# Input projection of a decoder trunk: both activation parts in one matmul stream, token scale folded into the operands, x and z in turn

## The chip, the cores and the metric

One core of one Trainium2 chip runs the whole program. The metric is device time in microseconds for one execution; three executions of the kernel before gave a median of 2697.6 us (2697.39 to 2698.57).

## What is computed

The reference is a two-layer decoder trunk over 256 tokens of width 2048: a Mamba-2 (SSD) mixer, a SwiGLU FFN, a dilated-window attention mixer and a second FFN, each behind an RMS norm and with a residual add. The change touches the first matrix product alone:

```python
h = rms_norm(x, mix_norm[0])          # x * gain * rstd(token)
proj = h @ w_in                       # 2048 -> 4096 (z) + 6144 (x, B, C) + 64 (dt)
xbc = silu(causal_depthwise_conv(proj_xbc, conv_w, conv_b))   # width 4
dt = softplus(dt_raw + dt_bias)
y = ssd_chunked(xs * dt, dt * a, b, c) + xs * d
y = group_rms_norm(y * silu(z), norm_w) @ w_out
```

## The kernel before, in words

**Number format.** Every fp32 operand is held as two fp32r parts, high and low. A product is weight-high times activation-high, weight-high times activation-low and weight-low times activation-high. Activations stand transposed, 128 channels by 256 tokens; `XT` holds the 16 blocks of 128 channels in 8 operand tiles, each block as `[high, low]` side by side, 512 columns in all.

**Weights.** They come from memory in tiles of 128x2048, each used as two *halves* of 1024 columns. `split` (line 145) makes a half's high part with a cast on ScalarE (ACT) and its low part with a subtraction on VectorE (DVE). There are four buffers for high and four for low parts, and `next_half` (line 160) splits three halves ahead. So while TensorE (PE) begins half n, the split of half n+3 is queued; its low part needs the buffer that half n-1 has just left. There are 914 halves, of which the input projection uses 162: 20 for each of the 8 head groups and 2 for `dt`.

**Products.** `t_unit`/`t_units` (lines 222 to 248) run 24 matmuls of 256 columns for a half (16 with the high weights, once for each activation part, and 8 with the low ones). `p_unit` (line 250) runs 8 matmuls of 512 columns, both activation parts in one stream, and 8 of 256; its two sums stand apart in PSUM, and `joined` (line 270) copies one on ACT and adds the other on DVE. Before the change p_units are used in both FFNs and in part of the output projections. Each unit has one of two PSUM accumulators: `begin_unit` (line 199) forces the evacuation of the unit two back.

**Order of the projection** (lines 633 to 643). Group g runs `bc` (B and C, 4 halves), in group 0 also `dt` (2 halves), then x (8 halves) and z (8 halves). The operands are x times gain, without the token scale `rb`, which is known only after the sum of squares; so every evacuation multiplies by `rb` on DVE (`scaled`, line 392).

**The rest is background work.** Evacuations, convolution (`first_tap` on ACT, `taps` on DVE, `half_tanh` on ACT, `gate` on DVE), the scan (`ssd`, line 532) and the group norm are Python generators in three queues: 0 for the evacuations and convolutions, 1 for norms, 2 for `dt` and `ssd`. After each half, `Background.step` (line 68) goes through the queues in that order and advances each by one `yield`, but only while its debt is low. The debt is counted in planner units, 0.1 plus elements/960 for a DVE instruction and 0.1 plus elements/1200 for an ACT one: 0.37 and 0.31 at 256 elements, 0.63 and 0.53 at 512. A step pays off 1.3 for DVE and 1.4 for ACT; a queue is passed over while the debt is above three quarters of these (0.975 for DVE). `Background.need` (line 74) advances all queues whatever the debt, until a wanted key is done. Splits are not counted in the debt. All engines take their instructions in the order in which the program wrote them.

```python
def step(self, free=False):
    self.debt = [max(d - s, -1.4) for d, s in zip(self.debt, self.SHARE)]
    for q in self.queues:
        if free or all(d < 0.75 * s for d, s in zip(self.debt, self.SHARE)):
            self.advance(q)
```

In the output projection the last group's operands are due 28 halves after the end of the input projection (`OUT0`, line 895).

Of the kernel before, what the change touches and what calls it, by code (L numbers as in the profile page):

```python
# [10 lines left out]
F32 = mybir.dt.float32  # L11
F32R = mybir.dt.float32r
AF = mybir.ActivationFunctionType
OP = mybir.AluOpType
AX = mybir.AxisListType

P = 128
S = 256
# [67 lines left out]
def trunk_kernel(  # L86
# [21 lines left out]
    def slot(shape, dt=F32):  # L108
        return slots.tile(shape, dt, tag="slot", bufs=28, name=name("slot"))
# [8 lines left out]
    def tmp(shape, dt=F32):  # L118
        return small.tile(shape, dt, tag="tmp", bufs=6, name=name("tmp"))
# [11 lines left out]
    bg = Background(3, (V, A))  # L131
# [115 lines left out]
    def t_unit(ncols, X, xkey, evac, q=0):  # L247
        t_units([(0, range(16))], ncols, 16, X, xkey, [evac], q)

    def p_unit(nk, X, xkey, evac):  # L250


        u, ps = begin_unit()
        for k0 in range(0, nk, 4):
            h, l = next_half(256)
            ks = range(k0, k0 + 4)
            for k in ks:
                bg.need((xkey, k // 2))
            for k in ks:
                for m in range(2):  # L260
                    T.matmul(ps[:, m], h[:, k % 4, m * P:(m + 1) * P], X[k], start=(k == 0), stop=False,  # L261
                             skip_group_check=True)
            for k in ks:
                for m in range(2):
                    T.matmul(ps[:, m, 0], l[:, k % 4, m * P:(m + 1) * P], X[k][:, 0, :], start=False,  # L265
                             stop=(k == nk - 1), skip_group_check=True)
            bg.step()
        bg.add(0, evac(ps, u))

    def joined(ps):  # L270
# [7 lines left out]
    XT = {}  # L278
# [60 lines left out]
    def clear_norm():  # L339
        bg.done -= {("XT", j) for j in range(8)} | {"rstd"}  # L340
        XT.clear()
# [10 lines left out]
    def t_residual(nb, gcol):  # L352
        def gen(ps, u):
            for b in range(2):
                k = 4 * nb + 2 * b
                V.tensor_tensor(xt[:, k:k + 2, :], ps[:, b], xt[:, k:k + 2, :], OP.add)
            bg.done.add(("evac", u))
            yield
            yield from after_residual((2 * nb, 2 * nb + 1), gcol)
        return gen  # L360
# [16 lines left out]
    def prep():  # L377
        for nb in range(4):
            for pair in (2 * nb, 2 * nb + 1):
                gained(pair, 0)  # L380
            add_squares()
            for pair in (2 * nb, 2 * nb + 1):
                squares(pair)
            yield
        yield from finish_norm()
        V.tensor_scalar(cwb, cwb, 0.5, None, OP.mult)
        A.activation(hpar[64:128, 1:2], hpar[64:128, 1:2], AF.Exp)
        V.tensor_scalar(hpar[64:128, 1:2], hpar[64:128, 1:2], -1.0, None, OP.mult)
        V.memset(hpar[0:64, 1:2], 1.0)
        bg.done.add("prep")  # L390

    def scaled(sums):
        u = tmp([P, 2, S])
        V.tensor_tensor(u, sums, rb[:, None, :].to_broadcast([P, 2, S]), OP.mult)
        return u

    def dt_evac(ps, u):
# [47 lines left out]
    def first_tap(u, dst, cts):  # L445

        for m, ct in enumerate(cts):
            A.activation(dst[:, m, :], u[:, m, :], AF.Identity, scale=cwb[:, 144 + ct:145 + ct],
                         bias=cwb[:, 192 + ct:193 + ct])

    def taps(u, dst, cts, js):
        for j in js:
            d = 3 - j
            for m, ct in enumerate(cts):
                V.scalar_tensor_tensor(dst[:, m, d:], u[:, m, :S - d], cwb[:, j * 48 + ct:j * 48 + ct + 1],
                                       dst[:, m, d:], OP.mult, OP.add)

    def half_tanh(v, scale):
        th = tmp([P, 2, S])
        A.activation(th, v, AF.Tanh, scale=scale)  # L460
        return th

    def gate(out_, th, v):
        V.scalar_tensor_tensor(out_, th, 1.0, v, OP.add, OP.mult)

    def bc_evac(g):
        def gen(ps, u):
            v = scaled(ps[:, :, 0])
            bg.done.add(("evac", u))
            yield  # L470
            both, cts = slot([P, 1024]), (32 + g, 40 + g)
            bc = both[:, 0:512].rearrange("p (a t) -> p a t", t=S)
            first_tap(v, bc, cts)
            yield
            taps(v, bc, cts, (2, 1))
            yield
            taps(v, bc, cts, (0,))
            yield
            th = half_tanh(bc, 1.0)
            yield  # L480
            gate(bc, th, bc)
            BC[g] = bc, both[:, 512:896]
            yield
        return gen

    def x_evac(g):
        def gen(ps, u):
            xs = slot([P, 4, S])
            d0, d1 = xs[:, 0:2, :], xs[:, 2:4, :]
            c0, c1 = (4 * g, 4 * g + 1), (4 * g + 2, 4 * g + 3)  # L490
            v0 = scaled(ps[:, 0])
            yield
            first_tap(v0, d0, c0)
            v1 = scaled(ps[:, 1])
            bg.done.add(("evac", u))
            yield
            taps(v0, d0, c0, (2, 1))
            first_tap(v1, d1, c1)
            yield
            taps(v0, d0, c0, (0,))  # L500
            taps(v1, d1, c1, (2,))
            yield
            th = half_tanh(d0, 1.0)
            taps(v1, d1, c1, (1, 0))
            yield
            gate(d0, th, d0)
            th = half_tanh(d1, 1.0)
            yield
            gate(d1, th, d1)
            XS[g] = xs  # L510
            bg.add(2, ssd(g))
        return gen

    def z_evac(g):
        def gen(ps, u):
            sz = slot([P, 4, S])
            v0 = scaled(ps[:, 0])
            yield
            t0 = half_tanh(v0, 0.5)
            v1 = scaled(ps[:, 1])  # L520
            bg.done.add(("evac", u))
            yield
            gate(sz[:, 0:2, :], t0, v0)
            t1 = half_tanh(v1, 0.5)
            yield
            gate(sz[:, 2:4, :], t1, v1)
            SZ[g] = sz
        return gen

    BC, XS, SZ, Y = {}, {}, {}, {}  # L530

    def ssd(g):
# [100 lines left out]
    bg.add(0, prep())  # L633
    bg.need(("XT", 1))
    for g in range(NG):
        t_unit(256, XT, "XT", bc_evac(g))
        if g == 0:
            t_unit(128, XT, "XT", dt_evac, 2)
        t_unit(512, XT, "XT", x_evac(g))
        t_unit(512, XT, "XT", z_evac(g))  # L640
    bg.need("rstd")
    bg.need(("evac", units[0] - 1))
    clear_norm()
    t_units(OUT0, 512, 32, Y, "Y", [t_residual(nb, 32) for nb in (0, 1)])
    for pair in range(4, 8):
        p_unit(32, Y, "Y", p_residual(pair, 32))
# [255 lines left out]
def _weights(i):  # L902


    w_in, w_out = np.asarray(i["ssm_w_in"])[0], np.asarray(i["ssm_w_out"])[0]
    w_qkv, a_out = np.asarray(i["attn_w_qkv"])[0], np.asarray(i["attn_w_out"])[0]
    gate, up, down = (np.asarray(i[n]) for n in ("ffn_w_gate", "ffn_w_up", "ffn_w_down"))
    halves = []

    def put(ks, *blocks):  # L910

        n = sum(b[2] for b in blocks)
        kk = 1024 // n
        for k0 in ks[::kk]:
            halves.append((k0, kk, blocks))

    r16 = range(16)
    for g in range(NG):
        put(r16, (w_in, 8192 + g * P, P), (w_in, 9216 + g * P, P))
        if g == 0:  # L920
            put(r16, (w_in, 10240, 64), (w_in, 10240, 64))
        put(r16, (w_in, 4096 + g * 512, 512))
        put(r16, (w_in, g * 512, 512))

    def put_out(w, order, nk):
        for j, ks in order:
            put(ks, (w, j * 512, 512))
        for pair in range(4, 8):
            put(range(nk), (w, pair * 256, 256))

    def put_ffn(l):
        for j in range(44):
            put(r16, (gate[l], j * P, P), (up[l], j * P, P))
        for pair in range(8):
            put(range(44), (down[l], pair * 256, 256))

    put_out(w_out, OUT0, 32)
    put_ffn(0)
    for hf, g, kind in QKV:
        put(r16, (w_qkv, ((g * 3 + kind) * 8 + hf * 4) * P, 512))  # L940
    put_out(a_out, OUT1, 8)
    put_ffn(1)
    packed = np.empty((len(halves) // 2, P, 2048), np.float32)
    for j, (k0, kk, blocks) in enumerate(halves):
        dst = packed[j // 2, :, (j % 2) * 1024:(j % 2 + 1) * 1024].reshape(P, kk, 1024 // kk)
        c = 0
        for w, c0, n in blocks:
            dst[:, :, c:c + n] = w[k0 * P:(k0 + kk) * P, c0:c0 + n].reshape(kk, P, n).transpose(1, 0, 2)
            c += n
    assert len(halves) % 2 == 0  # L950
    return packed
# [60 lines left out]
```

## Time and profile before

| what | value |
|---|---|
| median of three runs | 2697.6 us |
| profiled execution, its own time | 2698.51 us |
| its span, first to last instruction | 2696.4 us |
| TensorE busy | 2673.5 us (99%) |
| VectorE busy | 1700.7 us (63%) |
| ScalarE busy | 1326.3 us (49%) |
| mean granted TensorE clock | 0.999 |

2.1 us of the profiled execution lie outside its span. A busy PE says only that matmuls were in flight; how many were started in a stretch says more. In a timeline, the first column is the start in us, the second the length, and what stands in brackets is how long the engine was idle before and what ended that.

### The profile page before, as it was taken

To read this page: it belongs to the slowest core of one execution; us is meant where nothing else is said; L and a number is where in the kernel's file an instruction comes from. 1 tells how busy PE (TensorE), PEld (TensorE's weight loads), DVE (VectorE), ACT (ScalarE), POOL (GpSimd) and SP (SyncE) were. 2 spreads that over 40 slices of the span, in tenths; PEclk is the share of its full clock that TensorE was granted. 3 is DMA by queue.
4 is the path that set the end of the run, shared out by engine and by line. 5 is a ranking of instruction groups with operands and counts; after the bars stand their busy time and mean duration, and the time that the engine had idled before them with its cause. 6 is when DMAs were issued, how large, how long until landed. Compare 5 with 4: busy or idle time off the path is not lost.

```text
span 2696.4 us, 40315 instructions
## 1 busy us (share of the span) xinstructions
PE 2673.5 (99%) x16460; PEld 2391.9 (89%) x16460; DVE 1700.7 (63%) x2104; ACT 1326.3 (49%) x1947; POOL 199.8 (7%) x215
## 2 busy tenths in 40 slices
PE   7999999999999999999999999999999999999999
PEld 7999999999888888888888888888888888888888
DVE  6777777756566666665555777766666666665444
ACT  5666666654454444444444555544454444444332
POOL 1011111110000000000001330220000000000000
PEclk9999999999999999999999999999999999999999
DMA  5454555545555555555555554553455555555553
GB/s 222 178 184 175 187 179 189 177 177 187 188 188 188 188 188 187 189 189 193 190 189 203 183 186 152 185 185 141 156 188 188 188 188 188 188 188 194 197 198 128
DMA packets 71432, 495.75 MB, mean 184 GB/s; under 512 B 8320, under 2 KB 8704, under 8 KB 13008
## 3 DMA queue, kind: packets, MB, share of 16 engines
q1 hardware_dynamic: 68400, 483.81, 49.5%
q0 software_dynamic: 2848, 9.37, 1.1%
q8 instruction: 129, 2.11, 0.3%
q14 instruction: 55, 0.45, 0.1%
HBM read 490.99 MB, written 2.16 MB: 183 GB/s over the span
## 4 chain that ended last, share of the span: by engine, by line
PE 98%; ACT 1%; issue 0%; DVE 0%; POOL 0%; DMA 0%; SPq 0%; ACTq 0%; POOLq 0%
PE acc L261 39%; PE acc L240 21%; PE acc L265 20%; PE acc L217 15%; PE bg L588 1%; PE bg L754 0%; PE bg L787 0%; PE bg L860 0%; PE bg L549 0%; ACT wh L38 0%; ACT slot L38 0%; PE bg L324 0%; PE bg L784 0%; PE bg L862 0%; DMA xres<-in_x_dram 0%
## 5 line engine op out<-in xcount | busy, mean ns | idle before, releaser
L38 DVE TENSOR_TENSOR wl<-w,wh 128x1024 fp32r<-128x1024 f32 x914 | 1128.3, 1236 | 904.7 <-ACT wh L38 903.7
L38 ACT CAST wh<-w 128x1024 fp32r<-128x1024 f32 x914 | 955.5, 1047 | 1089.8 <-PE acc L261 507.2
L261 PE MATMUL acc<-slot,wh 128*128 128x512 f32 x4416 | 1106.7, 392 | 2.1 <-DVE xres L38 1.7
L261 PEld LDWEIGHTS acc<-slot,wh 128*128 128x128 f32 x4416 | 794.2, 189 | 145.1 <-issue 2.7
L265 PEld LDWEIGHTS acc<-slot,wl 128*128 128x128 f32 x4416 | 602.4, 190 | 43.0
L265 PE MATMUL acc<-slot,wl 128*128 128x256 f32 x4416 | 615.7, 282 | 0.0
L240 PE MATMUL acc<-slot,wh 128*128 128x256 f32 x3232 | 430.1, 286 | 12.8 <-ACT wh L38 10.7
L240 PEld LDWEIGHTS acc<-slot,wh 128*128 128x128 f32 x3232 | 404.8, 193 | 19.9 <-ACT wh L38 10.8
L217 PE MATMUL acc<-wh,slot 128*128 128x512 f32 x1152 | 290.5, 394 | 0.0
L217 PEld LDWEIGHTS acc<-wh,slot 128*128 128x128 f32 x1152 | 213.7, 188 | 43.2
L240 PE MATMUL acc<-slot,wl 128*128 128x256 f32 x1616 | 226.8, 283 | 0.9 <-DVE wl L38 0.9
L240 PEld LDWEIGHTS acc<-slot,wl 128*128 128x128 f32 x1616 | 208.6, 192 | 1.1 <-DVE wl L38 1.1
L217 PE MATMUL acc<-wl,slot 128*128 128x512 f32 x576 | 154.2, 389 | 0.0
L217 PEld LDWEIGHTS acc<-wl,slot 128*128 128x128 f32 x576 | 108.1, 188 | 22.7
L38 ACT ACTIVATE tmp<-tmp 128x256 f32<-128x256 f32 (+1 forms) x104 | 46.8, 450 | 163.9 <-DVE tmp L38 163.6
L284 POOL TENSOR_TENSOR tmp<-tmp 128x256 f32<-128x256 f32 x32 | 27.6, 868 | 1022.1 <-ACT tmp L38 1017.0
L38 ACT ACTIVATE wide<-tmp,bias 128x128 f32<-128x128 f32 x192 | 62.9, 391 | 13.9 <-PE bg L588 9.4
L38 DVE SCALAR_TENSOR_TENSOR slot<-tmp,vec,slot 128x255 f32<-128x255 f32 (+1 forms) x144 | 67.6, 528 | 0.0
L38 DVE TENSOR_TENSOR tmp<-tmp 128x256 f32<-128x256 f32 x88 | 37.4, 425 | 42.6 <-ACT tmp L38 42.6
L38 DVE TENSOR_TENSOR tmp<-acc,tmp 128x512 f32<-128x512 f32 x88 | 60.1, 683 | 4.0 <-ACT tmp L38 4.0
L38 DVE TENSOR_TENSOR tmp<-tmp,rb 128x512 f32<-128x512 f32 x88 | 60.3, 686 | 0.1
L38 ACT ACTIVATE tmp<-slot 128x128 f32<-128x128 f32 (+1 forms) x136 | 52.7, 394 | 14.9 <-DVE slot L38 13.8
(131 smaller groups left out, 1191.3 us busy)
## 6 DMA issues: line engine op xcount, KB each, us to landing
w<-in_weights_dram SPq DMA_DIRECT2D x455, 1024.0 KB, 4.8
tmp<-acum POOLq DMA_DIRECT2D x32, 256.0 KB, 4.6
xres<-in_x_dram SPq DMA_DIRECT2D x4, 512.0 KB, 7.8
w<-in_weights_dram SPq DMA_DIRECT2D x4, 512.0 KB, 8.4
out_dram<-xres SPq DMA_DIRECT2D x8, 256.0 KB, 2.2
slot<-in_mask_dram POOLq DMA_DIRECT2D x1, 384.0 KB, 5.6
slot<-in_q_norm_dram POOLq DMA_DIRECT2D x1, 192.0 KB, 5.6
slot<-in_k_norm_dram POOLq DMA_DIRECT2D x1, 192.0 KB, 7.5
```

The costliest lines, as they stand in the source:

```text
L38: return call(out, *args, **kw)
L217: T.matmul(ps[tb], X[k][:, part, tb * P:(tb + 1) * P], w[:, k % 2, :], start=(k == 0 and i == 0), stop=(k == 15 and i == 2))
L240: T.matmul(pss[j][:, b, c, :], w[:, k % kk, m * P:(m + 1) * P], X[k][:, part, :], start=(k == 0 and i == 0 and c == 0), stop=(k == nk - 1 ...
L261: T.matmul(ps[:, m], h[:, k % 4, m * P:(m + 1) * P], X[k], start=(k == 0), stop=False, skip_group_check=True)
L265: T.matmul(ps[:, m, 0], l[:, k % 4, m * P:(m + 1) * P], X[k][:, 0, :], start=False, stop=(k == nk - 1), skip_group_check=True)
L284: G.tensor_tensor(sq[:, 0, :], sq[:, 0, :], sq[:, 1, :], OP.add)
L588: T.matmul(o[:, tb * P:], xdt[:, tb, q * 64:(q + 1) * 64], m[:, 256 * tb:256 + 128 * tb], start=(tb == 0 and q % 4 < 2), stop=(tb == 1), s ...
```

## The change

- The projection uses `p_unit` for everything but `dt`; x and z are cut into two units each, in the order bc, x, z, x, z, four halves each. The weight packing follows that order.
- `total` takes the place of `scaled`: it joins the two sums (ACT copy, DVE add) and multiplies by `rb` in group 0 alone.
- From group 1 on the operands are `XN`, which hold gain and `rb`. `normed` makes them, in queue 1, in 16 advances that begin when the token scale is known: per pair of blocks two DVE instructions, then an ACT copy and a DVE subtraction.
- The convolution is one generator, `conv`, with fewer yields: `first_tap` follows `total` in the same advance, and `half_tanh` follows the last tap in the same advance.

```diff
@@ p_unit
-            bg.step()
+            bg.step(units[0] == 1)
@@ prep
         bg.done.add("prep")
-
-    def scaled(sums):
-        u = tmp([P, 2, S])
-        V.tensor_tensor(u, sums, rb[:, None, :].to_broadcast([P, 2, S]), OP.mult)
+        bg.add(1, normed())
+
+    XN = {}
+
+    def normed():
+        for pair in range(8):
+            v, t = tmp([P, 2, S]), operand()
+            for i in range(2):
+                k = 2 * pair + i
+                V.scalar_tensor_tensor(v[:, i, :], xt[:, k, :], gains[:, k:k + 1], rb, OP.mult, OP.mult)
+            yield
+            A.copy(t[:, :, 0, :], v)
+            V.tensor_tensor(t[:, :, 1, :], v, t[:, :, 0, :].bitcast(F32), OP.subtract)
+            store(XN, 2 * pair, t)
+            bg.done.add(("XN", pair))
+            yield
+
+    def total(ps, g):
+        u = joined(ps)
+        if g == 0:
+            V.tensor_tensor(u, u, rb[:, None, :].to_broadcast([P, 2, S]), OP.mult)
         return u
@@ evacuations
+    def conv(u, dst, cts, finish):
+        first_tap(u, dst, cts)
+        yield
+        taps(u, dst, cts, (2, 1))
+        yield
+        taps(u, dst, cts, (0,))
+        th = half_tanh(dst, 1.0)
+        yield
+        gate(dst, th, dst)
+        finish()
+
     def bc_evac(g):
         def gen(ps, u):
-            v = scaled(ps[:, :, 0])
+            v = total(ps, g)
             bg.done.add(("evac", u))
...
+            yield from conv(v, bc, (32 + g, 40 + g), finish)
         return gen
-    def x_evac(g):
+    def x_evac(g, i):
         def gen(ps, u):
...
+            v = total(ps, g)
             bg.done.add(("evac", u))
+            if i == 0:
+                XS[g] = slot([P, 4, S])
+
+            def finish():
+                if i == 1:
+                    bg.add(2, ssd(g))
+
+            yield from conv(v, XS[g][:, 2 * i:2 * i + 2, :], (4 * g + 2 * i, 4 * g + 2 * i + 1), finish)
         return gen
-    def z_evac(g):
+    def z_evac(g, i):
         def gen(ps, u):
...
+            v = total(ps, g)
             bg.done.add(("evac", u))
+            if i == 0:
+                sz[g] = slot([P, 4, S])
+            th = half_tanh(v, 0.5)
+            yield
+            gate(sz[g][:, 2 * i:2 * i + 2, :], th, v)
+            if i == 1:
+                SZ[g] = sz.pop(g)
         return gen
@@ main loop
-        t_unit(256, XT, "XT", bc_evac(g))
+        X, key = (XT, "XT") if g == 0 else (XN, "XN")
+        p_unit(16, X, key, bc_evac(g))
         if g == 0:
             t_unit(128, XT, "XT", dt_evac, 2)
-        t_unit(512, XT, "XT", x_evac(g))
-        t_unit(512, XT, "XT", z_evac(g))
-    bg.need("rstd")
+        for c in range(4):
+            p_unit(16, X, key, (x_evac if c % 2 == 0 else z_evac)(g, c // 2))
+        if g == 0:
+            XT.clear()
     bg.need(("evac", units[0] - 1))
     clear_norm()
+    XN.clear()
@@ _weights
-        put(r16, (w_in, 4096 + g * 512, 512))
-        put(r16, (w_in, g * 512, 512))
+        for i in range(2):
+            put(r16, (w_in, 4096 + g * 512 + i * 256, 256))
+            put(r16, (w_in, g * 512 + i * 256, 256))
```

## Rows read from the trace of the kernel before

**Rows 1.** The profile's page: busy time by engine, the chain that ended last.

```profile
PE 2673.5 (99%) x16460; PEld 2391.9 (89%) x16460; DVE 1700.7 (63%) x2104; ACT 1326.3 (49%) x1947; POOL 199.8 (7%) x215
PE 98%; ACT 1%; issue 0%; DVE 0%; POOL 0%; DMA 0%; SPq 0%; ACTq 0%; POOLq 0%
```

**Rows 2.** Waits of PE by releaser, from 0 to 520 us.

```profile
PE acc L240 <- ACT wh L38: 10.7, 1, 10.7
PE bg L324 <- POOL tmp L321: 2.3, 1, 2.3
PE acc L240 <- DVE tmp L38: 1.8, 1, 1.8
```

**Rows 3.** Windows: busy us (instructions) of each engine, granted clock, DMA share, GB/s.

```profile
100.00:150.00 50.00, 50.00 (x418) 48.16 (x417) 39.55 (x57) 33.37 (x60) 6.56 (x7) 1.00 0.49 180
450.00:500.00 50.00, 50.00 (x417) 48.99 (x416) 39.66 (x60) 32.33 (x55) 8.74 (x10) 1.00 0.52 187
900.00:1000.00 100.00, 100.00 (x575) 88.03 (x574) 61.22 (x73) 47.59 (x63) 0.00 (x0) 1.00 0.52 189
```

**Rows 4.** PE timeline, t_unit halves in the projection: first and last of seven starts.

```profile
62.27 2.08 PE L240 MATMUL acc<-slot,wh 128*128 128x256 f32 x16
64.19 1.12 PE L240 MATMUL acc<-slot,wl 128*128 128x256 f32 x8
...
79.55 0.64 PE L240 MATMUL acc<-slot,wh 128*128 128x256 f32 x4
```

**Rows 5.** PE timeline, p_unit halves: first and last of six starts.

```profile
632.73 2.00 PE L261 MATMUL acc<-slot,wh 128*128 128x512 f32 x8
634.57 1.11 PE L265 MATMUL acc<-slot,wl 128*128 128x256 f32 x8
...
646.70 0.63 PE L261 MATMUL acc<-slot,wh 128*128 128x512 f32 x2
```

**Rows 6.** Groups of instructions on DVE and ACT, 100 to 500 us.

```profile
L38 DVE TENSOR_TENSOR wl<-w,wh 128x1024 fp32r<-128x1024 f32 x126 | 157.9, 1253 | 96.9 <-ACT wh L38 96.8
L38 DVE TENSOR_TENSOR tmp<-acc,rb 128x512 f32<-128x512 f32 x31 | 21.2, 683 | 0.0
L38 DVE TENSOR_TENSOR slot<-slot,slot 128x512 fp32r<-128x512 f32 x12 | 7.7, 682 | 0.0
L38 DVE TENSOR_TENSOR slot<-bg,cm 128x128 f32<-128x128 f32 x12 | 2.9, 282 | 0.0
L38 ACT CAST wh<-w 128x1024 fp32r<-128x1024 f32 x126 | 131.6, 1045 | 118.1 <-PE acc L240 110.1 <-issue 6.4 <-ACT slot L38 0.8
L38 ACT CAST slot<-slot 128x512 fp32r<-128x512 f32 x12 | 6.8, 612 | 0.0
```

**Rows 7.** ACT groups of the first FFN, 660 to 1150 us.

```profile
L38 ACT COPY tmp<-acc 128x512 f32<-128x512 f32 x38 | 22.0, 580 | 0.0
L38 ACT ACTIVATE tmp<-tmp 128x256 f32<-128x256 f32 x37 | 15.5, 418 | 68.8 <-DVE tmp L38 68.8
```

**Rows 8.** Timeline of a convolution and its scan, 439 to 463 us.

```profile
439.07 1.23 DVE L38 TENSOR_TENSOR wl<-w,wh 128x1024 fp32r<-128x1024 f32 x1 [1.54 <-ACT wh L38]
440.21 0.55 DVE L38 TENSOR_TENSOR wide<-wide,slot 128x384 f32<-128x384 f32 x1
441.72 0.87 PE L588 MATMUL bg<-wide,slot 128*64 128x256 f32 x8
...
460.71 1.65 DVE L38 SCALAR_TENSOR_TENSOR slot<-tmp,vec,slot 128x254 f32<-128x254 f32 x4
460.87 0.51 PE L311 MATMUL bg<-ones,tmp 128*128 128x2 f32 x4
462.45 0.63 ACT L38 ACTIVATE tmp<-slot 128x512 f32<-128x512 f32 x1 [1.29 <-DVE slot L38]
```

**Rows 9.** PE timeline: the same sum of squares, one group later.

```profile
524.77 0.51 PE L311 MATMUL bg<-ones,tmp 128*128 128x2 f32 x4
```

**Rows 10.** Windows as in rows 3, around the wait for the token scale.

```profile
35.00:40.00 5.00, 3.23 (x13) 2.54 (x13) 1.23 (x4) 2.73 (x6) 0.00 (x0) 0.50 0.00 0
40.00:45.00 5.00, 5.00 (x40) 5.00 (x39) 4.54 (x5) 3.88 (x6) 0.00 (x0) 0.88 0.26 90
```

**Rows 11.** PE timeline: the first half after that wait, high weights, then low.

```profile
37.56 3.75 PE L240 MATMUL acc<-slot,wh 128*128 128x256 f32 x16 [1.77 <-DVE tmp L38]
41.11 1.17 PE L240 MATMUL acc<-slot,wl 128*128 128x256 f32 x8
```

More of the change, by code (lines that the diff above doesn't have):

```diff
@@ L464, in gate @@
         V.scalar_tensor_tensor(out_, th, 1.0, v, OP.add, OP.mult)
+    def conv(u, dst, cts, finish):
[8 more added lines that the diff above has]
+        finish()
     def bc_evac(g):
         def gen(ps, u):
-            v = scaled(ps[:, :, 0])
+            v = total(ps, g)
             bg.done.add(("evac", u))
-            yield
-            both, cts = slot([P, 1024]), (32 + g, 40 + g)
@@ L472, in gen @@
[L472 to L483, printed above, removed]
-        return gen
-    def x_evac(g):
[L487 to L512, printed above, removed]
@@ L514, in z_evac @@
-    def z_evac(g):
[L515 to L528, printed above, removed]
+            both = slot([P, 1024])
+            bc = both[:, 0:512].rearrange("p (a t) -> p a t", t=S)
@@ new lines, in finish, with gen @@
+            def finish():
+                BC[g] = bc, both[:, 512:896]
+            yield from conv(v, bc, (32 + g, 40 + g), finish)
+        return gen
+    def x_evac(g, i):
+        def gen(ps, u):
+            v = total(ps, g)
+            bg.done.add(("evac", u))
+            if i == 0:
+                XS[g] = slot([P, 4, S])
+            def finish():
+                if i == 1:
+                    bg.add(2, ssd(g))
+            yield from conv(v, XS[g][:, 2 * i:2 * i + 2, :], (4 * g + 2 * i, 4 * g + 2 * i + 1), finish)
+        return gen
@@ L530, in trunk_kernel, with gen @@
+    def z_evac(g, i):
+        def gen(ps, u):
+            v = total(ps, g)
+            bg.done.add(("evac", u))
+            if i == 0:
+                sz[g] = slot([P, 4, S])
+            th = half_tanh(v, 0.5)
+            yield
+            gate(sz[g][:, 2 * i:2 * i + 2, :], th, v)
+            if i == 1:
+                SZ[g] = sz.pop(g)
+        return gen
+    sz = {}
     BC, XS, SZ, Y = {}, {}, {}, {}
```

## The prediction

> **What bounds the kernel now.** The page comes first: PE is busy 99% of the span, and the chain that ended last lies on PE for 98% [rows 1]. The reader should see that only two things move the time: how fast PE gets through a half, and whether it waits. Next, PE's waits over the projection: 14.8 us in three rows, all at the start, where the first weights and the token scale are late [rows 2]; from 45 us on PE never waits. Then the windows: in the projection DVE is busy 39.6 of 50 us and ACT 33, in the FFN only 61 and 48 of 100 [rows 3]. The projection is the stage with the least slack behind PE, and that is where the change puts more work. Last, the pace of a half: seven t_unit starts lie 17.28 us apart, so a half takes 2.880 us [rows 4]; six p_unit starts lie 13.97 us apart, 2.794 us [rows 5].
>
> **The change, part by part.**
>
> *Pairing.* 160 halves become p_units; the first four are paced by casts at the start, so 156 gain 2.880 - 2.794 = 0.086 us: **-13.5 us**. The columns streamed are the same; what is saved is the spacing, 0.230 us for one matmul of 512 (1.84 us for 8) [rows 5] against two of 0.120 (1.92 us for 16) [rows 4]. The Trainium skill ("TensorE: Matmul & The Clock Gate", Back-to-back issue gap) puts 262 cycles on 256 columns and 518 on 512, at 2.4 GHz 2.5 ns less for one wide matmul than for two narrow ones. By that the pairing would give an estimated 3.1 us in place of 13.5, and the sum below would be 10 us higher; here the trace has both shapes, and it decides.
>
> *Evacuations.* `scaled`, one DVE instruction of 0.683 us, becomes an ACT copy of 0.580 us and a DVE add of the same shape as before [rows 6, 7]. From group 1 on DVE is even and ACT gains 5 x 0.58 = 2.9 us a group; group 0 pays five more multiplies, 3.4 us of DVE. At the one place where PE waits for an evacuation today, the third row there [rows 2], the copy goes ahead of the add: **+0.7 us**.
>
> *normed.* Sixteen DVE instructions of 0.41, eight of 0.68 and eight ACT copies of 0.61 (four taps take 1.65 us) [rows 6, 8]: 12 us of DVE and 5 of ACT, hidden if done by half 22, where group 1 begins. I stepped the planner by its own costs. A convolution's advance of four taps costs 1.47 units, above the 0.975 limit, so on those steps queue 1 is passed over. XN pair 0 is stored in the step after half 13, pair 1 after 16, pair 2 after 21. Group 1's first half needs pairs 0 and 1, its second pairs 2 and 3, and so on: pairs 3 to 7 are forced in halves 23, 24 and 25, and each forced round also advances `dt` in queue 2.
>
> A forced round costs PE time for this reason: it is written after the split of half n+3, whose low part waits for the buffer that half n-1 leaves, so DVE gets to the forced work only when PE already stands at half n. From there to XN pair 7, DVE has 3 low parts (3.75 us), 10 products (4.1), 5 subtractions (3.4), a gate (0.7), 15 `dt` instructions of 256 (6.2) and two of 128 (0.6): 18.7 us [rows 6, 8]. Two ACT copies that nothing covers add 1.2, and PE's last pair and low part 1.9, with about 0.7 of waiting in between: 22.5 us for three halves of 2.79, so PE loses 14. That is with engines on time, the lower bound. In halves 6 to 22 DVE has 17 low parts (21.3), three convolutions with join and scale (13.6), a z and a half (3.4), three pairs (4.6) and the head of `dt` (3): 46 us against 17 x 2.79 = 47.5. It is full and will come late. Stepping the three in-order queues with these durations and carrying the lag gives 24, the upper end. I take the middle: **+19**.
>
> *The debt.* That burst leaves it at 12.8 units. At 1.3 a half, plain steps stay shut for the rest of group 1, and evacuations come only when `begin_unit` forces them, in order behind what stands ahead of them in queue 0 and beside the scan. Before half 34, for instance, DVE has to do a low part (1.25), six taps (2.5), the scan's scaling (1.9), a gate and the add (1.4), with a tanh, the scan's four ACT instructions and the copy between (about 2.9 exposed): 9.2 us from the start of half 33 where 2.8 are free, a stall of 6.4. By the same count half 38 costs 5.1 and half 46 2.9; 30 and 42 nothing, since there the add is nearly first and beats PE. Sum 14; where PE has already stalled the engines have caught up, so the bounds are 8 and 15, and I take **+13**.
>
> *Steady groups 2 to 7.* Today's group takes 63.9 us (the sum-of-squares matmul at 460.87 and 524.77) [rows 8, 9], 57.6 of halves and 6.3 of scan matmuls; paired it would be 62.2. But ACT, in order, is now blocked in each of five evacuations from its copy until DVE has done its low part and the add, since `first_tap` or tanh follows in the same advance, and in each of three convolutions from the last tap to the tanh. Prices: the FFN's joined units block ACT 68.8/37 = 1.86 us each [rows 7], with a multiply more; a tanh behind taps 1.29 [rows 8]. I take 1.3 for all eight: 10.4 us a group. ACT then has 33 x 63.9/50 = 42 [rows 3], plus 2.9, plus 10.4: 55.5 of 62.2 us busy or blocked, and while it is blocked no cast runs, so DVE's next low part is late too. What becomes late is the scan: its matmuls on PE (at 441.72) need a multiply that DVE does one half earlier (at 440.21) [rows 8], with some 2 us to spare. No row shows this stall. It is bounded by 0 (every block covered) and 10.4 (every one passed on). Stepping the queues, lags of 3 to 8 us build up around the scan's first steps and PE waits two or three times a group, 2 to 4 us each: I take 7, **+42 for six groups**.
>
> *At no cost.* The last group's operands come some 21 halves into the output projection where 28 are allowed; without that margin PE would wait for them outright. Weight bytes and SyncE's issues stay the same; POOL gets nothing new but waits behind the scan. Eight more operand tiles live during group 0, with room among 28.
>
> Sum: -13.5 + 0.7 + 19 + 13 + 42 = +61 us. The profiled execution took 2698.5; 2760 for its like, and the median lies 0.9 lower: **2759 us**.
>
> **The rivals.**
>
> *A. Only group 1 pays.* If the casts' lead of three halves covers ACT's blocks, the steady term is near 0: -13.5 + 0.7 + 14 to 24 + 8 to 15, so +9 to +26, about 2715 us. For it: today DVE still waits 97 us for casts in 400 us [rows 6], which is slack. Against it: 55.5 of 62.2 on ACT.
>
> *B. The clock falls too.* When PE idled before half 6, its granted clock went to 0.50, the lower level of 1.2 GHz, and was still 0.88 on average in the next window [rows 10]; 16 matmuls of 256 columns then took 3.55 us for 1.92 [rows 4, 11]. Three half-idle halves around 23 and repeated stalls could do that again: 2 us for each of 3 to 12 stalls, 2765 to 2785.
>
> *C. Faster.* The prices stand, but the order is kinder: DVE reaches `normed` early because real durations undercut the planner's (four taps 1.65 us for 1.47 units speaks against it), and ACT's blocks fall in time it now spends waiting for PE (118 us in 400 [rows 6]). Then only the pairing is left: 2685 us. It decides at half 22: all eight XN pairs must be stored by then without force, five more than I count.
>
> *D. No change.* The pairing pays for group 1 and the rest is covered: 2693 to 2703.
>
> **How the numbers follow.** Forecast with steady stalls, +30 to +80: 0.58. A 0.19, B 0.09, C 0.09, D 0.05. A measurement of this kernel can tell about 0.2%, 5.4 us, from no change: faster 0.09, same 0.05, slower 0.86. For the range I leave out C, D and the upper end: from the foot of A, 2707, up to the sum with the clock's price, 2786. The bounds of the terms alone (steady 0 to 62, XN 14 to 24, forced 8 to 15) reach from +9 to +98.
>
> **What would show it.** Right: p_unit halves at 2.79 us in the projection; between some 80 and 115 us PE waiting for `slot` operands from DVE; waits for `acc` releases in the group after; scan matmuls (L588 before) waiting for `wide` in every group; ACT's idle before tmp and slot instructions, ended by DVE, up from 12 us in 400 to some 60. Wrong: PE busy throughout from 45 us on, or XN stored before half 22; then A to D. If groups 2 to 7 take 62 us each, the steady term failed; if group 1 is also 62, the planner was read wrongly.

## The result, and the profile after

The changed kernel takes **2775.2 us** (2774.35 to 2777.01), the kernel before 2698.1 on the same chips: a ratio of 1.0287, 95% interval 1.0269 to 1.0305. It is 77 us slower; 2759 was forecast, with a range of 2707 to 2786. The profiled execution spans 2772.5 us, 76.1 more than before.

From its page, the busy times, the chain that ended last and the granted clock in 40 slices:

```profile
PE 2690.8 (97%) x15180; PEld 2343.1 (85%) x15180; DVE 1715.1 (62%) x2133; ACT 1344.6 (48%) x1995; POOL 206.3 (7%) x215
PE 89%; DVE 4%; ACT 3%; issue 2%; DMA 0%; POOL 0%; DVEq 0%; ACTq 0%; SPq 0%; POOLq 0%
PEclk9799999999999999999999999999999999999999
```

PE has 1280 matmuls fewer than in [rows 1], and the chain leaves it for a tenth of the span. DVE and ACT have hardly more to do, 14 and 18 us. So the loss is not work but waiting, and the next view is PE's waits by releaser up to 640 us (total us, times, longest):

```profile
PE bg L594 <- DVE wide L38: 17.0, 7, 5.6
PE acc L261 <- DVE slot L38: 15.2, 5, 6.0
PE acc L261 <- DVE tmp L38: 13.5, 4, 6.1
PE acc L261 <- ACT wh L38: 10.9, 1, 10.9
PE bg L555 <- DVE slot L38: 9.4, 3, 3.1
PE bg L452 <- DVE tmp L38: 3.5, 1, 3.5
```

Only the 10.9 us for the first weights and 2.1 of the third row are old [rows 2]; 0.8 of the second row lies at the start too. The second row is projection matmuls waiting for their operands, the third accumulators that are not yet evacuated, the first and fifth the scan, the sixth `dt`. Cut by stage, with the times at which PE starts halves 22, 26, 42 and so on in the two timelines:

| stage | before, us | after, us | difference |
|---|---|---|---|
| halves 6 to 21 (group 0) | 48.0 | 47.3 | -0.7 |
| halves 22 to 25 (group 1, bc) | 14.5 | 40.3 | +25.8 |
| halves 26 to 41 (rest of group 1) | 52.0 | 61.7 | +9.7 |
| groups 2 to 7, 20 halves each | 64.3, 63.7, 63.9, 63.9, 63.9, 63.9 | 73.4, 69.3, 70.9, 71.0, 68.9, 69.4 | +39.3 |
| before half 6, and after the projection | | | +2.0 |

What happens in halves 22 to 25 is seen in the timeline of all engines; the brackets say how long the engine was idle and what ended that:

```profile
87.01 1.11 PE L265 MATMUL acc<-slot,wl 128*128 128x256 f32 x8
...
90.66 0.68 DVE L38 SCALAR_TENSOR_TENSOR slot<-tmp,slot 128x512 f32<-128x512 f32 x1
90.85 0.57 ACT L38 COPY tmp<-acc 128x512 f32<-128x512 f32 x1
91.26 0.68 DVE L38 TENSOR_TENSOR slot<-tmp,slot 128x512 fp32r<-128x512 f32 x1
91.86 1.22 DVE L38 TENSOR_TENSOR wl<-w,wh 128x1024 fp32r<-128x1024 f32 x1
92.00 2.07 PE L261 MATMUL acc<-slot,wh 128*128 128x512 f32 x4 [3.88 <-DVE slot L38]
...
99.36 0.68 DVE L38 TENSOR_TENSOR slot<-tmp,slot 128x512 fp32r<-128x512 f32 x1
...
100.10 2.07 PE L261 MATMUL acc<-slot,wh 128*128 128x512 f32 x4 [6.03 <-DVE slot L38]
...
101.97 1.91 PE L265 MATMUL acc<-slot,wl 128*128 128x256 f32 x8
...
103.99 1.23 DVE L38 TENSOR_TENSOR wl<-w,wh 128x1024 fp32r<-128x1024 f32 x1 [2.82 <-PE acc L265]
```

The DVE subtractions at 91.26 and 99.36 make XN pairs 2 and 3, and PE starts four matmuls 0.06 us after each is done. The last line shows the return path: the next low part waits for PE to leave its buffer, so DVE can't work ahead while PE waits for DVE. The other thing to see is the length: four matmuls of 512 take 1.87 us from start to start, where eight take 1.84 elsewhere. The clock had fallen (windows as in rows 3):

```profile
95.00:100.00 5.00, 0.00 (x0) 0.00 (x0) 3.93 (x8) 1.62 (x3) 0.00 (x0) 0.50 0.43 184
110.00:115.00 5.00, 4.21 (x14) 3.44 (x14) 2.38 (x6) 1.04 (x1) 0.00 (x0) 0.50 0.00 0
125.00:130.00 5.00, 5.00 (x28) 4.37 (x27) 2.45 (x2) 1.19 (x2) 0.25 (x1) 0.97 0.83 274
```

A stall of a steady group, from the same timeline:

```profile
243.69 0.99 ACT L38 ACTIVATE wide<-tmp,bias 128x128 f32<-128x128 f32 x3 [3.68 <-DMA tmp<-acum]
...
245.14 1.04 ACT L38 CAST wh<-w 128x1024 fp32r<-128x1024 f32 x1
246.08 0.58 ACT L38 COPY tmp<-acc 128x512 f32<-128x512 f32 x1
246.21 1.23 DVE L38 TENSOR_TENSOR wl<-w,wh 128x1024 fp32r<-128x1024 f32 x1 [4.31 <-ACT wh L38]
247.35 0.68 DVE L38 TENSOR_TENSOR tmp<-acc,tmp 128x512 f32<-128x512 f32 x1
...
248.07 1.09 ACT L38 ACTIVATE slot<-tmp,vec 128x256 f32<-128x256 f32 x2 [1.41 <-DVE tmp L38]
248.79 0.65 PE L594 MATMUL bg<-wide,slot 128*64 128x256 f32 x2
249.07 0.97 ACT L38 ACTIVATE wide<-tmp,bias 128x128 f32<-128x128 f32 x3
...
250.50 1.03 ACT L38 CAST wh<-w 128x1024 fp32r<-128x1024 f32 x1
...
251.56 1.22 DVE L38 TENSOR_TENSOR wl<-w,wh 128x1024 fp32r<-128x1024 f32 x1 [3.06 <-ACT wh L38]
...
254.35 0.55 DVE L38 TENSOR_TENSOR wide<-wide,slot 128x384 f32<-128x384 f32 x1
254.81 1.22 DVE L38 TENSOR_TENSOR wl<-w,wh 128x1024 fp32r<-128x1024 f32 x1
255.04 1.51 PE L594 MATMUL bg<-wide,slot 128*64 128x256 f32 x6 [5.61 <-DVE wide L38]
```

Read it from the bottom. PE waits 5.61 us for the scan's multiply of 254.35. DVE comes to it late because its low part waited 3.06 us for ACT's cast of 250.50; ACT was late with that because first_tap, at 248.07, had stood 1.41 us behind DVE's add, which itself lay behind the low part of 246.21, late by a cast. That is the loop that the merged advances close: ACT waits for DVE, then DVE for ACT. The first line shows how this lag began: the cast of 245.14 was late because ACT had stood 3.68 us at the scan's own transfer. Such waits for a transfer make 4.5 us of ACT's 400 here (100 to 500 us) and none in the run of the merged advances alone, below, whose groups are as long; so the steady loss does not rest on them.

### The profile page after: what moved, and what is told of

The parts are those of the page before. It is cut to its first block, busy times and chain, and to the rows that moved or that the text cites. A ratio compares the mean times of both kernels' runs of the same rounds, so it can differ in the third digit from the quotient of the medians.

```text
span 2772.5 us, 37850 instructions
## 1 busy us (share of the span) xinstructions
PE 2690.8 (97%) x15180; PEld 2343.1 (85%) x15180; DVE 1715.1 (62%) x2133; ACT 1344.6 (48%) x1995; POOL 206.3 (7%) x215
## 4 chain that ended last, share of the span: by engine, by line
PE 89%; DVE 4%; ACT 3%; issue 2%; DMA 0%; POOL 0%; DVEq 0%; ACTq 0%; SPq 0%; POOLq 0%
PE acc L261 45%; PE acc L265 23%; PE acc L217 14%; PE acc L240 4%; DVE slot L38 2%; ACT wh L38 1%; DVE wl L38 1%; PE bg L594 1%; ACT wide L38 1%; ACT slot L38 1%; DVE tmp L38 1%; ACT tmp L38 0%; PE bg L763 0%; PE bg L796 0%; PE bg L869 0%
## 5 line engine op out<-in xcount | busy, mean ns | idle before, releaser
L261 PE MATMUL acc<-slot,wh 128*128 128x512 f32 x5696 | 1450.3, 397 | 42.1 <-DVE slot L38 15.2
L261 PEld LDWEIGHTS acc<-slot,wh 128*128 128x128 f32 x5696 | 1034.8, 191 | 237.7 <-issue 21.0
L265 PEld LDWEIGHTS acc<-slot,wl 128*128 128x128 f32 x5696 | 782.2, 192 | 57.2 <-DVE wl L38 0.7
L265 PE MATMUL acc<-slot,wl 128*128 128x256 f32 x5696 | 798.5, 283 | 0.2 <-DVE wl L38 0.2
L38 DVE TENSOR_TENSOR tmp<-acc,tmp 128x512 f32<-128x512 f32 x128 | 87.4, 683 | 8.0 <-ACT tmp L38 8.0
L240 PE MATMUL acc<-slot,wh 128*128 128x256 f32 x672 | 90.0, 287 | 0.0
L240 PEld LDWEIGHTS acc<-slot,wh 128*128 128x128 f32 x672 | 85.2, 195 | 0.9 <-issue 0.7
L38 ACT COPY tmp<-acc 128x512 f32<-128x512 f32 x128 | 74.2, 579 | 5.4 <-PE acc L265 5.3
L594 PE MATMUL bg<-wide,slot 128*64 128x256 f32 (+1 forms) x256 | 36.0, 348 | 17.3 <-DVE wide L38 17.0
```

The costliest lines, as they stand in the source:

```text
L38: return call(out, *args, **kw)
L240: T.matmul(pss[j][:, b, c, :], w[:, k % kk, m * P:(m + 1) * P], X[k][:, part, :], start=(k == 0 and i == 0 and c == 0), stop=(k == nk - 1 ...
L594: T.matmul(o[:, tb * P:], xdt[:, tb, q * 64:(q + 1) * 64], m[:, 256 * tb:256 + 128 * tb], start=(tb == 0 and q % 4 < 2), stop=(tb == 1), s ...
```

## Experiments

Each kernel is timed against the kernel before on the same chip; "groups" are the times from the start of halves 6, 22, 42, ... 142 to the next, group 0 without its first six halves. Edits are against the changed kernel. The theory is the prediction's three parts: XN late, the debt after it, merged advances in every group.

**Without XN.**

```diff
-        X, key = (XT, "XT") if g == 0 else (XN, "XN")
+        X, key = XT, "XT"
-        bg.add(1, normed())
     def total(ps, g):
-        if g == 0:
-            V.tensor_tensor(u, u, rb..., OP.mult)
+        V.tensor_tensor(u, u, rb..., OP.mult)
```

> The changed kernel without XN: every group uses the unscaled operands and every evacuation multiplies by the token scale on DVE (0.69 us more in each of 35 units). My theory (late XN, the debt it leaves, and merged advances that block ACT in every group): the wait for operands and the forced evacuations of group 1 go, but the steady groups keep 68 to 76 us each where 62.2 are due, as the merged advances stay and DVE has more to do; about 2755 to 2780 us. Rival 1 (late XN and its debt are nearly all of the loss, the rest is aftermath): about 2695 to 2705 us. Rival 2 (join, pairing and short units load ACT and DVE too much whatever the order): as mine here, 2755 or more.

Measured: 2753.6 us, ratio 1.0205 (1.019 to 1.022). Groups 47.2, 70.5, 68.9, 69.3, 70.7, 68.8, 73.6, 79.3. Group 1 loses its burst, 101.9 to 70.5, and all others stay bad. Late XN alone is not the loss.

**Yields back.**

```diff
     def conv(u, dst, cts, finish):
+        yield
         first_tap(u, dst, cts)
...
         taps(u, dst, cts, (0,))
+        yield
         th = half_tanh(dst, 1.0)
@@ z_evac
+            yield
             th = half_tanh(v, 0.5)
```

> The changed kernel with its XN, but with three yields back: between the join and first_tap, between the last tap and the tanh, and between the join and the tanh of z. Same instructions, another order. My theory: group 1 still loses 20 to 35 us and the debt lasts longer, since there are more advances; from group 4 or 5 on the groups run at 62 to 63 us with PE waiting for nothing; about 2725 to 2750 us. Rival 1 (late XN alone): group 1 as bad as in the changed kernel, and no gain from the yields in the later groups, about 2770 us. Rival 2 (the amount of work): the later groups stay at 69 us, about 2770 us.

Measured: 2734.2 us, 1.0136 (1.0121 to 1.0151). Groups 50.8, 83.8, 81.8, 65.3, 63.7, 62.7, 62.2, 65.9: two bad groups, a recovery, and then the 62 that pairing should give, with XN and every instruction in place. So the amount of work is not the cause, the order is.

**Both.**

> Both at once: no XN, every evacuation scales, and the three yields are back. What is left of the change is the paired streams, the join and the order x, z, x, z. My theory: every group takes 62 to 62.5 us, PE waits for nothing after 45 us, and the pairing's gain is seen: 2685 to 2693 us, faster than before. Rival 1: as e1, about 2695. Rival 2 (the join's extra copy and add, with 35 more multiplies, are what DVE and ACT cannot carry): the groups stay near 69 us, 2750 us or more.

Measured: **2687.3 us, 0.996 (0.9946 to 0.9975), faster than the kernel before**, by 0.4%. Groups 47.1, 63.0, 62.8, 62.3, 62.4, 61.3, 62.2, 64.9. PE's waits up to 660 us are the start's again, but for the last row, 0.4 us of the scan:

```profile
PE acc L261 <- ACT wh L38: 11.0, 1, 11.0
PE bg L324 <- POOL tmp L321: 2.3, 1, 2.3
PE acc L261 <- DVE tmp L38: 2.1, 1, 2.1
PE acc L261 <- DVE slot L38: 0.8, 1, 0.8
PE acc L265 <- DVE wl L38: 0.6, 1, 0.6
PE bg L556 <- DVE slot L38: 0.4, 1, 0.4
```

What ACT waited for from 100 to 500 us tells the same. First the changed kernel, then this one:

```profile
ACT tmp L38 <- DVE slot L38: 60.8, 16, 5.9
ACT slot L38 <- DVE tmp L38: 41.7, 20, 4.1
ACT wh L38 <- PE acc L261: 38.6, 30, 3.1
```

```profile
ACT wh L38 <- PE acc L261: 93.7, 72, 3.0
...
ACT slot L38 <- DVE tmp L38: 5.9, 9, 1.7
ACT tmp L38 <- DVE slot L38: 5.8, 6, 1.5
```

Here ACT waits for PE to leave a weight buffer, as before the change [rows 6]; in the changed kernel it waits for DVE.

**The merged advances alone**, on the products and the scaling of the kernel before:

```diff
-        p_unit(16, X, key, bc_evac(g))
+        t_unit(256, X, key, bc_evac(g))
...
-        u = joined(ps)
+        u = tmp([P, 2, S])
+        V.tensor_tensor(u, ps[:, :, 0], rb..., OP.mult)
```

with the same for x and z, and no XN.

> The kernel before's products and scaling (24 matmuls of 256 columns a half, no join, no XN) in the changed kernel's order of units and with its merged advances: less work than the changed kernel on ACT and DVE, and no pairing. My theory: the merged advances alone make steady stalls, groups of 68 to 72 us where 63.9 are due, with PE waiting for the scan's multiply; about 2735 to 2755 us. Rival 1 and rival 2 (late XN, or the amount of work): 63.9 us a group and about 2698 us, as before.

Measured: 2738.4 us, 1.0152 (1.0135 to 1.0169). Groups 47.7, 70.7, 68.4, 70.8, 69.4, 70.9, 69.4, 71.2. With less work on ACT than the changed kernel and no pairing, the merges alone cost 36.5 us against the same kernel with the three yields (2701.9 us, below). PE's waits, up to 660 us:

```profile
PE bg L553 <- DVE slot L38: 17.4, 7, 2.7
PE bg L592 <- DVE wide L38: 7.5, 7, 1.4
```

**Which merge?** From the run without XN, first only the two yields after the join are given back:

> As the run without XN and with merged advances (2753.6 us), with two of the three yields back: between the join and first_tap and between the join and the tanh of z; the convolution's tanh stays in the advance of the last tap. Theory: each merge lets ACT stand behind DVE, five a group for the join, three for the tanh, and lags add up faster than in proportion; undoing the five gets most back: groups of 62 to 67 us, 2690 to 2715 us. Rival (blocks count alike, about 8 us for each kind of three): some 2725 us.

Measured: 2708.6 us, 1.0038 (1.0023 to 1.0053). Groups 47.0, 63.6, 64.7, 66.0, 65.0, 66.0, 66.3, 66.7.

Then only the one before the tanh:

> The other half: no XN, only the yield between the last tap and the tanh is back, the joins stay merged with first_tap and with the tanh of z. Theory: five blocks a group remain, groups of 63 to 70 us, 2715 to 2745 us. Rival (the tanh behind the taps is the costly one, since four taps and a low part stand ahead of it): 2690 to 2700 us.

Measured: 2735.9 us, 1.0139 (1.0124 to 1.0154). Groups 46.6, 69.4, 70.2, 72.2, 70.4, 69.1, 69.9, 65.9. Against 2753.6 the five joins give back 45.0 us and the three tanhs 17.6; together they gave 66.3. So the parts nearly add up, about 1.1 us for each join (45.0 over 8 groups of 5) and 0.7 for each tanh. That lags grow faster than in proportion, as the expectation had it, was not shown. A yield also puts all that follows it one step later; no run here separates that from the block that it takes away.

**XN due one group later.**

```diff
-        X, key = (XT, "XT") if g == 0 else (XN, "XN")
+        X, key = (XT, "XT") if g < 2 else (XN, "XN")
-        if g == 0:
+        if g < 2:
             V.tensor_tensor(u, u, rb..., OP.mult)
```

with `XT` kept to the end of group 1.

> The changed kernel with XN used from group 2 on, not from group 1: groups 0 and 1 use XT and scale, all merges as in the change. It takes the due date of XN away, 20 halves later, and nothing else. Theory: group 1, 101.9 us in the changed kernel, falls to 65 to 72 us, groups 2 to 7 stay at 67 to 76; 2745 to 2765 us. Rival (the steady stalls are aftermath of group 1's burst): all groups near 62, about 2695 us.

Measured: 2739.6 us, 1.0153 (1.0137 to 1.0168). Groups 47.5, 62.1, 70.9, 74.3, 71.1, 67.1, 74.5, 71.6. The due date alone is worth 35.7 us, more than I expected: group 1 has 4.3 us of waits for casts and no wait for an operand, and the timeline shows none of the scan's matmuls in it: the scan is put off, for `dt`, which stands ahead of it in queue 2, reaches its transposes only in half 46. Groups 2 to 7 are as bad as ever, so they are not the burst's aftermath.

**The order of the units**, in the run with neither XN nor merges:

```diff
-            p_unit(16, X, key, (x_evac if c % 2 == 0 else z_evac)(g, c // 2))
+            p_unit(16, X, key, (x_evac if c < 2 else z_evac)(g, c % 2))
```

with the weights packed to match.

> The run without XN and with all three yields (2687.3 us), in the order x, x, z, z instead of x, z, x, z. Theory: what costs is the order inside the advances, not of the units; 2683 to 2692 us. Rival (alternation spreads the convolutions' DVE work and without it two convolutions in a row put DVE behind): 2700 us or more.

Measured: 2687.6 us, 0.9961 (0.9947 to 0.9975), the same as with alternation (2687.3).

**XN from group 2, join apart.** The two edits above together, the tanh still merged.

> XN kept, but used from group 2 on, and the join apart from what follows it on ACT (the tanh stays behind the last tap). Theory: the two causes are separate and both mended here, save for three tanh blocks a group; with 30 multiplies fewer on DVE than the run with the same yields and no XN (2708.6 us), groups of 62 to 66 us; 2690 to 2705 us. Rival (making XN on DVE and ACT in groups 0 and 1 costs as much as the multiplies it saves): 2706 to 2715 us.

Measured: 2693.3 us, 0.9982 (0.9973 to 0.9992), faster than before. Groups 47.5, 55.9, 64.5, 63.4, 66.1, 64.1, 63.4, 67.4. Against 2708.6 for the same yields without XN, the scaled operands do save: 15 us. They help when they aren't due in a hurry. ACT's waits from 100 to 500 us set a limit to the reading of ACT above:

```profile
ACT tmp L38 <- DVE slot L38: 54.3, 18, 5.4
ACT wh L38 <- PE acc L261: 39.1, 31, 2.9
...
ACT slot L38 <- DVE tmp L38: 7.7, 7, 1.7
```

ACT's tanh stands behind DVE's taps nearly as long as in the changed kernel, and ACT waits for PE's buffers as little as there (38.6 us); yet PE waits only 4.3 us after half 6. What fell is the third row, `first_tap` behind the join, from 41.7 us (9.8 of them `normed`'s copies) to 7.7. So ACT's waiting for DVE is not a loss by itself; it is one where PE then waits too.

**The pairing by itself.** The fourth run's products with all three yields.

> The kernel before's products (24 matmuls of 256, scaled on the way out of PSUM) in units of four halves, x, z, x, z, with all three yields: the run without XN and with the yields (2687.3 us), less the pairing and the join. It prices the pairing by itself. Theory: 63.9 us a group and 2697 to 2701 us, as the kernel before; so the pairing is worth 10 to 14 us (13.5 by my sum). Rival (the gain came from the shorter units, not from the pairing): about 2687 us.

Measured: 2701.9 us (2700.0 to 2703.3), 1.0012 (1.0003 to 1.0022), just above the expected band; groups 2 to 6 at 63.9 each. Against 2687.3 the pairing, its join paid for, is worth 14.6 us. In its profiled execution one wait of 2.5 us for POOL in the last group, which the run with pairing doesn't show, is part of that; groups 2 to 6 differ by 1.7 us each, or 13.6 over eight groups.

**The debt set to zero** in each round forced for XN:

```diff
     def need(self, key):
...
             for q in self.queues:
                 self.advance(q)
+            if key[0] == "XN":
+                self.debt = [min(d, 0.0) for d in self.debt]
```

> The changed kernel, with the debt set to zero or less after each round that was forced for XN: later steps are not shut, and no evacuation of group 1 has to be forced by the debt. Theory as in the prediction (the debt costs 13 us of its own): group 1 falls from 101.9 to about 90 us, 2760 to 2765 us. Rival (the work has to be done anyway; open steps put it on DVE and ACT at once, and the scan waits instead of the accumulators): 2770 to 2780 us, waits for acc releases replaced by waits for wide.

Measured: 2770.1 us (2764.6 to 2773.5), 1.0264 (1.0249 to 1.028). Group 1 falls from 101.9 to 94.3 us, the others keep 69 to 72. The median lies at the foot of the rival's band, but two of the four runs lie below it, so the time alone doesn't decide. PE's waits up to 660 us, of which the last row is now the start's alone (line numbers are two higher):

```profile
PE bg L557 <- DVE slot L38: 22.0, 7, 3.2
PE acc L263 <- DVE slot L38: 13.6, 5, 6.0
...
PE acc L263 <- DVE tmp L38: 2.1, 1, 2.1
```

The waits for accumulators are gone, 11.4 us in the changed kernel beyond the start's 2.1. The scan's waits, for `slot` and `wide` together, go from 26.4 to 31.1 us; the rival had named `wide`, and it is `slot` that grows.

## Why the prediction was right, and where its sizes were off

**Direction and place: right; the total in part by luck.** PE waits where it was said to, for operands in halves 23 and 24 and for `dt` before 25, for accumulators before halves 34, 38 and 46, for the scan in groups 2 to 7, and rivals A, C and D fell: groups 2 to 7 take 69 to 73 us, not 62. The time lies in rival B's band too, 2765 to 2785, and B's clock was there. The sum put 74 us on waits (19 + 13 + 42) and nothing on the clock. PE waited 58 us (17.9 + 11.4 + 28.8, below); the clock, some 21 us by the estimates below, and 8 us that I can't assign made up for it. Two of its sums are off: the items listed for half 34 add up to 9.95 us, not 9.2, and the bounds of the terms reach to +88, not +98.

**Pairing, -13.5 us.** Measured 14.6 in the pair of runs, up to 2.5 of it one wait for POOL. A half takes 2.79 us in the projection too, as these two starts of group 0, 13 halves and 36.31 us apart, show:

```profile
46.06 2.00 PE L261 MATMUL acc<-slot,wh 128*128 128x512 f32 x8
...
82.37 2.00 PE L261 MATMUL acc<-slot,wh 128*128 128x512 f32 x8
```

The 3.1 us that went by the Trainium skill ("TensorE: Matmul & The Clock Gate", Back-to-back issue gap) were too little; the measurement decides.

**Evacuations, +0.7 us.** PE's wait before half 6 grew from 1.8 us [rows 2] to 2.1, by 0.3.

**XN, +19 us: mechanism right, too small.** PE waited 3.88 + 6.03 + 3.57 + 0.91 for operands and 3.51 for `dt`, 17.9 us, inside the 14 to 24. The 3.88 is for pair 2, which was not forced: its subtraction, at 91.26, stands before the low part of 91.86, which is half 25's and is written at the start of half 22; so it was written in the step after half 21, as planned, and DVE came to it late, as the count of 46 us of work in 47.5 had it. But the four halves took 40.3 us where four halves (11.2) and the twelve small `dt` matmuls (some 1.4 before the change) take some 12.6 at full clock; 28 were lost, so by estimate 10 came from the matmuls themselves, at the clock of 0.50. That price I had set apart as rival B and not in the sum.

**The debt, +13 us: the step that failed as I put it.** The stalls came, 6.1 before half 34, 3.3 before half 38 and 2.0 before half 46, 11.4 us for 13. But the debt is not their price: with it cleared the kernel gained 5 us in the median (2 to 11 over the four runs), not 13. The waits for accumulators went, and the scan's grew by 4.7 us. That the burst's work has to be done anyway, so that open steps only move a part of the wait, fits this but is not shown by itself.

**Steady groups, +42 us: right in kind, too small in all, too large for the waits.** Net of pairing 39.3 us were lost; with its 1.72 us a group that makes 49.6. PE's idle time in this stretch, in these windows, is 9.8 + 21.0 us:

```profile
187.00:260.00 73.00, 63.24 (x362) 53.76 (x359) 45.22 (x69) 40.15 (x70) 12.38 (x11) 0.95 0.44 154
260.00:610.00 350.00, 328.99 (x1899) 278.79 (x1897) 253.82 (x374) 217.45 (x387) 63.22 (x65) 0.98 0.47 167
```

The 2.0 before half 46 is among them and is the debt's, which leaves 28.8 us, 4.8 a group where 7 were put down. Clocks of 0.95 and 0.98 account for some 11 more by estimate (73 x 0.05 + 350 x 0.02). About 8 us I can't assign. The estimate of ACT's blocks, 10.4 us a group, was low: the two rows ended by DVE above make 102.5 us in 400, some 18 us in a group of 70, of which slack covers more than half.

**What hid the cost from a glance at the page.** DVE is busy 62% and ACT 48%, with one point less than before each. These shares don't show an order problem; PE's waits show that there is one, and the releasers of ACT's idle time where to look.

## What to carry to other kernels

When two in-order engines hand work to each other and both also feed the bottleneck, leave a step between producing a value on one and using it on the other; three yields were worth 41 us here, without one instruction less, and 66 us in the kernel without XN. When an operand is prepared in the background for a known due date, count the steps that its queue will get until then, not the work; due 20 halves later, the same operands cost 36 us less. And look at what the waiting engine waits for, before and after: an ACT that waits for PE's buffers is ahead, one that waits for DVE has used up slack, and whether that costs time PE's own waits tell.

## What was unexpected

The clock was part of the price. In the windows from 95 to 115 us, PE was busy 0.00 to 4.21 of each 5 us, and its clock stayed at 0.50, the lower level of 1.2 GHz. It averaged 0.84 in the window from 115, was 0.50 once more in the one from 120, with PE busy all 5 us, and 0.97 in the one from 125. Over the run the mean was 0.987 for 0.999 before. Waits of 17.9 us thus cost some 28.

Two further things: the order x, z, x, z, which looks like the heart of the change, was worth nothing (0.3 us); and XN, which cost 22 us with the merges in place (2775.2 against 2753.6) and 47 without them (2734.2 against 2687.3), gains 15 us once it is due later, with the tanh still merged. Where no merge is left, PE waits 0.4 us after half 6, so there is next to nothing for XN to save, and no run has it due later there. The merges cost more than XN in either pairing, 41 us with it and 66 without.
